# The first stage of a hybrid block in a new written order: two row loads moved, values by halves, roots and exponential steps on GpSimd

## The chip, the cores and the metric

The kernel runs on one core of a Trainium2 chip. Its time is the device time of one execution in microseconds. It has five engines that work side by side, each through its own queue in order: TensorE (PE: matmuls, with weight loads shown as PEld), VectorE (DVE), ScalarE (ACT), GpSimd (POOL) and SyncE (SP), which here issues the loads and stores. They wait for each other through semaphores.

## The reference, cut to what matters

One layer of a model with 512 tokens of width 1024. It norms the input, multiplies it by a wide matrix, runs a state-space branch and an attention branch with compressed, selected and window keys on the result, merges them, and goes on to a feed-forward part and to a gate on a second embedding `p`:

```python
n1 = rmsnorm(h, g_mix[i])
z = n1 @ w_in[i]
y_ssm = s5_mixer(z[..., OFF_SSM:OFF_Q], ...)
y_nsa = nsa_mixer(z[..., OFF_Q:OFF_KV], ...)
...
gate = jax.nn.sigmoid(rmsnorm(h, g_ple[i]) @ w_ple_gate[i])
h = h + gate * (p[i] @ w_ple_proj[i])
```

Three pieces of it are made in the first stage of the kernel: `p @ w_ple_proj` (512x256 by 256x1024), which needs nothing else; the normed input `n1`; and the columns of `z` that hold the attention values and gates (280 of them). The norm is `x * rsqrt(mean(x*x) + eps) * g`. The state-space branch also needs `exp(lam * dt)`, whose modulus is `rho = exp(lr)` with `lr = lre * dt`, and whose angle goes through sine and cosine tables.

## The kernel before, in words

Every fp32 matrix is split in a high part, which TensorE takes as fp32r, and a low part, the rest. A product is three passes: high by high, low by high, high by low. ScalarE copies the high part and VectorE (later in the kernel GpSimd as well) subtracts it to get the low one.

Tokens stand in four tiles of 128 (`qt` 0 to 3), the width in eight blocks of 128 (`k`). The input is loaded twice: as rows (`rows[qt]`, a token on each partition) and transposed (`xT[:, qt]`, the width on the partitions). For a tile, the first stage does this:

- `squared` (L314): ScalarE squares the row and sums it on the way.
- `rooted` (L318 to L322): GpSimd adds eps and raises to the power -0.5, the sum of one tile at a time.
- `spread` (L324): TensorE multiplies the 128 roots by a diagonal matrix, so that they stand along the free dimension of a bank, the same on all partitions.
- `x_scaled` (L329): VectorE multiplies each block of `xT` by its column of gains and by the spread roots, four blocks a half.
- `n_high`, `n_low`: ScalarE copies the high part into `n1h` by halves, VectorE subtracts it to get `n1l` in one instruction a tile.
- `v_passes` (L290): TensorE multiplies the normed tile by the value weights `WV` (high and low, made by `copy(*wv(...))` and `wv_lo`), three passes of eight matmuls.

Ahead of them and between them TensorE does `embedded(i, qt)` (L426): the product of `p` with the half `i` of `w_ple_proj`, six matmuls of 512 columns for each of the eight (`i`, `qt`). `embedded_out` copies each result out of its bank; SyncE stores it to DRAM later. VectorE has small steps besides: `angles()` (L391), a generator of 128x16 instructions that `some(n)` advances, ends with the angle of the state-space poles and gives `lr` after sixteen steps. `exp_of(rho, lr, "e1", G)` gives `rho` on GpSimd, after the stage, where the planner puts it behind `exp_at`. `u_split` splits the weights of the first two projections.

Two rules set the order. Inside `tc.manual_schedule` (L445 to L529) the instructions of TensorE, ScalarE, VectorE and GpSimd keep the order in which they are written, each engine its own. Everything outside is placed by a planner that orders the queues by its own costs; `tc.issue_after(ins)` keeps a block's instructions behind `ins` on its engine. Loads on SyncE keep their written order at the head of the program. Banks of PSUM come in four pairs (`acc`, `s`, `t`, `o`); a matmul into a pair waits until an older user of a bank is read out. `either()` hands out `acc` and `o` in turn.

After the stage, the first of the projections (`proj`, 24 matmuls of 512 columns) multiplies `n1` by 128 columns of `w_in`. It needs all four tiles of `n1h` and `n1l`, and so everything above.

## Time and profile before

| | us |
|---|---|
| median of three runs | 806.93 (806.4 to 807.37) |
| the profiled execution | 806.35 |
| its span, first instruction to last | 804.6 |
| TensorE busy in the span | 789.8 |
| VectorE, ScalarE, GpSimd busy | 515.6, 403.4, 251.0 |
| start of the first projection's matmuls | 34.59 |

Rows of the profile give the start and the length in us, the engine, the line of the kernel, the operation and its output and inputs by name; x8 stands for eight such instructions in a row; the bracket tells how long the engine sat idle before and what ended that. Rows of groups give the busy time and the mean ns of one, then the idle time in front of the group. Rows by stretch give the stretch's length and then each engine's busy time with its count of instructions, the granted TensorE clock, the share of DMA and GB/s. Rows of DMA issues give KB and the us from issue to landing. Most of these operations stand on helper lines (L54 is any `tt`, L58 and L60 any `ts`, L63 any `stt`, L75 any `copy`), so the tile's name tells which it is.

### The profile page before, as it was taken

The page shows a single profiled execution, that of the slowest core. Times are in us where ns is not written, and L with a number is a line of the kernel's source. Part 1 is how long each engine was busy: PE and PEld are TensorE (multiplying, and loading weights), DVE is VectorE, ACT ScalarE, POOL GpSimd, SP SyncE. Part 2 cuts the span into 40 slices and gives each one's busy share as a digit, 9 for nine tenths or more (in the row PEclk, how much of TensorE's full clock was granted, in tenths as well). Part 3 has the DMA queues.
Part 4 walks back from the last instruction along what each step waited for, and adds up shares of the span by engine and source line. Part 5 has one row for each costly group of instructions (what it writes and reads, how often), then busy time and mean ns, then how long its engine had stood idle before and what let it go on. Part 6 is the DMA issues. An engine that isn't in the chain of part 4 may idle for free.

```text
span 804.6 us, 12045 instructions
## 1 busy us (share of the span) xinstructions
PE 789.8 (98%) x4432; PEld 665.4 (83%) x4432; DVE 515.6 (64%) x1082; ACT 403.4 (50%) x747; POOL 251.0 (31%) x289
## 2 busy tenths in 40 slices
PE   8999999999999999999999999999999999999996
PEld 7888888878888888878898888888888888888885
DVE  6898996866677732595454444545544757999753
ACT  6735653366776743344363444443443433584642
POOL 1667222117555534141032333223333200001221
PEclk9999999999999999999999999999999999999999
DMA  9953212133413312334032222233222252515111
GB/s 349 340 178 131 79 52 73 50 105 105 106 54 107 144 60 83 106 131 156 1 132 95 89 105 82 102 105 105 82 102 98 94 174 80 209 66 171 54 52 53
DMA packets 29851, 89.70 MB, mean 111 GB/s; under 512 B 3680, under 2 KB 6112, under 8 KB 29792
## 3 DMA queue, kind: packets, MB, share of 16 engines
q1 hardware_dynamic: 29216, 87.88, 32.1%
q10 hardware_dynamic: 576, 1.05, 0.3%
q8 instruction: 35, 0.57, 0.3%
q14 instruction: 24, 0.20, 0.1%
HBM read 79.48 MB, written 5.24 MB: 105 GB/s over the span
## 4 chain that ended last, share of the span: by engine, by line
PE 90%; DVE 5%; ACT 2%; issue 2%; DMA 0%; POOL 0%; POOLq 0%; ACTq 0%; DVEq 0%
PE pj L82 6%; PE pj L83 6%; PE pj L84 6%; PE ua L83 5%; PE ub L84 5%; PE ua L84 5%; PE ua L82 5%; PE ub L82 5%; PE ub L83 5%; PE p L82 3%; PE p L83 3%; PE p L84 3%; PE sps L1020 2%; PE ptp L1040 2%; PE wo L82 2%; PE wo L83 2%
## 5 line engine op out<-in xcount | busy, mean ns | idle before, releaser
L54 POOL TENSOR_TENSOR wl<-wr,wh 128x1024 fp32r<-128x1024 f32 x39 | 93.7, 2403 | 249.4 <-ACT wh L75 215.7
L75 ACT ACTIVATE wh<-wr 128x1024 fp32r<-128x1024 f32 x88 | 93.2, 1059 | 91.4 <-issue 35.0
L54 DVE TENSOR_TENSOR wl<-wr,wh 128x1024 fp32r<-128x1024 f32 x49 | 64.1, 1309 | 51.9 <-ACT wh L75 51.7
L82 PE MATMUL pj<-n1h,wh 128*128 128x512 f32 x224 | 90.7, 405 | 0.9 <-ACT hid L871 0.6
L83 PE MATMUL pj<-n1l,wh 128*128 128x512 f32 x224 | 87.8, 392 | 0.0
L84 PE MATMUL pj<-n1h,wl 128*128 128x512 f32 x224 | 87.4, 391 | 0.0
L63 DVE SCALAR_TENSOR_TENSOR cv<-ub,cols,cv 128x511 f32<-128x511 f32 (+1 forms) x44 | 32.9, 748 | 66.1 <-ACT cv L1312 65.4
L83 PE MATMUL ua<-n2l,wh 128*128 128x512 f32 (+1 forms) x176 | 66.9, 380 | 0.2 <-DVE n2l L63 0.2
L82 PE MATMUL ua<-n2h,wh 128*128 128x512 f32 (+1 forms) x176 | 66.9, 380 | 0.0
L83 PE MATMUL ub<-n2l,wh 128*128 128x512 f32 (+1 forms) x176 | 66.8, 379 | 0.0
L84 PE MATMUL ub<-n2h,wl 128*128 128x512 f32 (+1 forms) x176 | 66.8, 379 | 0.0
L82 PE MATMUL ub<-n2h,wh 128*128 128x512 f32 (+1 forms) x176 | 66.8, 379 | 0.0
L84 PE MATMUL ua<-n2h,wl 128*128 128x512 f32 (+1 forms) x176 | 66.8, 379 | 0.0
L82 PEld LDWEIGHTS pj<-n1h,wh 128*128 128x128 f32 x224 | 42.1, 188 | 9.4 <-ACT hid L871 0.7
L84 PEld LDWEIGHTS pj<-n1h,wl 128*128 128x128 f32 x224 | 42.1, 188 | 8.9
L83 PEld LDWEIGHTS pj<-n1l,wh 128*128 128x128 f32 x224 | 42.2, 188 | 7.7 <-issue 0.4
L60 POOL TENSOR_SCALAR pr<-pr,su,gates 128x512 f32<-128x512 f32 (+2 forms) x64 | 40.3, 644 | 16.7 <-DVE su L1032 13.2
L54 DVE TENSOR_TENSOR pl<-ptp,ph 128x128 fp32r<-128x128 f32 (+1 forms) x64 | 31.0, 487 | 16.4 <-ACT ph L75 15.2
L75 ACT ACTIVATE ph<-ptp 128x128 fp32r<-128x128 f32 (+1 forms) x64 | 27.7, 435 | 26.9 <-PE ptp L1040 26.7
L83 PEld LDWEIGHTS ua<-n2l,wh 128*128 128x128 f32 x176 | 33.1, 188 | 6.7 <-DVE n2l L63 0.4
L84 PEld LDWEIGHTS ub<-n2h,wl 128*128 128x128 f32 x176 | 33.1, 188 | 6.3
L84 PEld LDWEIGHTS ua<-n2h,wl 128*128 128x128 f32 x176 | 33.1, 188 | 6.2
(481 smaller groups left out, 2014.5 us busy)
## 6 DMA issues: line engine op xcount, KB each, us to landing
wr<-in_w_up_dram SPq DMA_DIRECT2D x44, 512.0 KB, 3.5
wr<-in_w_in_dram SPq DMA_DIRECT2D x28, 512.0 KB, 3.4
b<-in_w_down_dram SPq DMA_DIRECT2D x14, 512.0 KB, 3.6
QQ<-QT SPq DMA_DIRECT2D x16, 256.0 KB, 3.8
wr<-in_w_out_dram SPq DMA_DIRECT2D x8, 512.0 KB, 3.5
wr<-in_w_down_dram SPq DMA_DIRECT2D x8, 512.0 KB, 3.9
wr<-in_w_ple_gate_dram SPq DMA_DIRECT2D x8, 512.0 KB, 3.5
xT<-in_x_t_dram SPq DMA_DIRECT2D x4, 512.0 KB, 9.0
```

The costliest lines, as they stand in the source:

```text
L54: e.tensor_tensor(o, a, b, op=op)
L60: e.tensor_scalar(o, a, s1, s2, op0=op0, op1=op1)
L63: e.scalar_tensor_tensor(o, a, s, b, op0=op0, op1=op1)
L75: S.activation(o, a, AF.Copy)
L82: PE.matmul(ps, lh, rh, start=start, stop=False)
L83: PE.matmul(ps, lh, rl, start=False, stop=False)
L84: PE.matmul(ps, ll, rh, start=False, stop=stop)
L1020: PE.matmul(o, self.QQ[:, x, qt * P:(qt + 1) * P], KK[:, :, self.g, :w] if both else KK[:, self.br, self.g, :w], start=x == 0, stop=x == 1)
L1040: PE.transpose(ps[:, (qt - kt) * P:(qt - kt + 1) * P], self.pr[qt][:, kt * P:(kt + 1) * P], ident)
```

## The change

- Warming: nine matmuls on a tile `heat`, filled by VectorE, in place of six on `ident` and `root`.
- Loads: rows 0 and 1 are issued behind the two loads of the second half of `w_ple_proj`; before, they were issued ahead of them. In both versions they are ahead of the first transposed tile.
- `spread` takes a bank for each tile, not one for all four. The banks of `embedded` and of the value products are named, not handed out in turn.
- `n_low` goes by halves. `v_pass` takes one pass, or half of one; the order of the passes differs from tile to tile, and a tile's passes no longer stand together.
- Tile 3's second half is scaled in two steps: GpSimd multiplies by the gains (`x_times_g`), then VectorE multiplies all four blocks by the spread roots in one instruction.
- Seven GpSimd instructions of the exponential are written after the roots of tiles 0 and 1; the rest after tile 3's gains, inside the written block. Before, all were behind `exp_at`.
- One copy out of a bank (`embedded_out(0, 2)`) is VectorE's. The copies out of banks, the square sums and the value weights come at other places.
- `v_high` and `v_low` of tiles 0 and 1 come after all low parts.
- Outside the block: `FL`'s and `CT`'s copies on ScalarE are held behind the last value copy, and `W2d`'s on GpSimd behind the tables.

```diff
@@ -236,8 +236,10 @@
     rows = [wv0[:, 1].rearrange("p a b -> p (a b)"), *(px.tile([P, D], F32, name=f"row{qt}") for qt in range(1, NQ))]
     root = px.tile([P, P], F32, name="root")
     ts(root, ident, math.sqrt(D), None, MUL, None, G)
-    half = px.tile([P, 1], F32, name="half")
-    G.memset(half, -0.5)
+    heat = px.tile([P, P], F32, name="heat")
+    V.memset(heat, 1.0)
+    expo = px.tile([P, 1], F32, name="expo")
+    G.memset(expo, -0.5)
 
     def rowload(qt):
         nc.sync.dma_start(rows[qt], dr("x", qt * P * D, [[D, P], [1, D]]))
@@ -259,10 +261,10 @@
         nc.sync.dma_start(pin[:, k], dr("p_t", k * T * P, [[T, P], [1, T]]))
         wpload(0, k)
     nc.sync.dma_start(cols, dr("cols", 0, [[NCOLS, P], [1, NCOLS]]))
-    for qt in range(2):
-        rowload(qt)
     for k in range(2):
         wpload(1, k)
+    rowload(0)
+    rowload(1)
     xload(0)
     VV = slot(pa, "v8", [P, NQ, 2, 2, 2, HD], F32R, "VV")
     WV = slot(pa, "kv", [P, 2, KD, 280], F32R, "WV")
@@ -287,14 +289,16 @@
     def wv_lo(i):
         tt(wv(1, i)[0], wv(1, i)[1], wv(0, i)[0], SUB)
 
-    def v_passes(qt, passes):
+    vcount = [0] * NQ
+
+    def v_pass(qt, n, ks=range(KD)):
         if qt not in vps:
-            vps[qt] = bank(either(), "vps")
-        for n in passes:
-            nn, x = ((n1h, 0), (n1l, 0), (n1h, 1))[n]
-            for k in range(KD):
-                PE.matmul(vps[qt][:, :280], nn[:, k, qt * P:(qt + 1) * P], WV[:, x, k], start=n + k == 0,
-                          stop=n == 2 and k == KD - 1)
+            vps[qt] = bank("ot"[qt // 2] if qt != 1 else "acc", "vps")
+        nn, x = ((n1h, 0), (n1l, 0), (n1h, 1))[n]
+        for k in ks:
+            PE.matmul(vps[qt][:, :280], nn[:, k, qt * P:(qt + 1) * P], WV[:, x, k], start=vcount[qt] == 0,
+                      stop=vcount[qt] == 3 * KD - 1)
+            vcount[qt] += 1
 
     def v_high(qt):
         S.activation(gates[:, qt], vps[qt][:, 256:280], AF.Tanh, scale=0.5)
@@ -319,33 +323,32 @@
 
         r = rx[qt] = small("rx")
         ts(r, ss4[:, qt:qt + 1], D * EPS, None, ADD, None, G)
-        tt(r, r, half, ALU.pow, G)
+        tt(r, r, expo, ALU.pow, G)
 
     def spread(qt):
-        if not rbp:
-            rbp[0] = bank("s", "rb")
-        PE.matmul(rbp[0][:, qt * P:(qt + 1) * P], rx[qt].to_broadcast([P, P]), root, start=True, stop=True)
+        rbp[qt] = bank("s", "rb")
+        PE.matmul(rbp[qt][:, :P], rx[qt].to_broadcast([P, P]), root, start=True, stop=True)
+
+    def x_times_g(qt, half):
+        for k in range(4 * half, 4 * half + 4):
+            ts(xT[:, qt, k], xT[:, qt, k], gmix[:, k:k + 1], e=G)
 
     def x_scaled(qt, half):
+        if qt == 3 and half:
+            x = xT[:, qt, 4 * half:4 * half + 4]
+            tt(x, x, rbp[qt][:, None, :P].to_broadcast([P, 4, P]), MUL)
+            return
         for k in range(4 * half, 4 * half + 4):
-            stt(xT[:, qt, k], xT[:, qt, k], gmix[:, k:k + 1], rbp[0][:, qt * P:(qt + 1) * P], MUL, MUL)
-
-    def n_of(qt, half):
-        ks = slice(4 * half, 4 * half + 4)
-        return (slice(None), ks, slice(qt * P, qt * P + P)), xT[:, qt, ks]
+            stt(xT[:, qt, k], xT[:, qt, k], gmix[:, k:k + 1], rbp[qt][:, :P], MUL, MUL)
+
+    def n_of(x, qt, half):
+        return x[:, 4 * half:4 * half + 4, qt * P:qt * P + P]
 
     def n_high(qt, half):
-        o, x = n_of(qt, half)
-        copy(n1h[o], x)
-
-    def n_low(qt):
-        o = (slice(None), slice(None), slice(qt * P, qt * P + P))
-        tt(n1l[o], xT[:, qt], n1h[o], SUB)
-
-    def normed_tile(qt):
-        for half in range(2):
-            x_scaled(qt, half)
-            n_high(qt, half)
+        copy(n_of(n1h, qt, half), xT[:, qt, 4 * half:4 * half + 4])
+
+    def n_low(qt, half):
+        tt(n_of(n1l, qt, half), xT[:, qt, 4 * half:4 * half + 4], n_of(n1h, qt, half), SUB)
 
     uw = []
 
@@ -425,28 +428,31 @@
 
     def embedded(i, qt, passes=range(3), ks=range(2)):
         if (i, qt) not in pjb:
-            pjb[i, qt] = bank("t" if i and qt < 2 else either(), "pje")
+            pjb[i, qt] = bank("t" if i and qt < 2 else ("o", "acc")[qt % 2], "pje")
         for k in ks:
             for n in passes:
                 PE.matmul(pjb[i, qt], pT[int(n == 1)][:, k, qt * P:(qt + 1) * P], wp[i][:, int(n == 2), k], start=n + k == 0,
                           stop=n + k == 3)
 
-    def embedded_out(i, qt):
+    def embedded_out(i, qt, e=None):
         n = 4 * i + qt
-        if n == 0:
+        if not pjs:
             pjs.append(slot(pa, "v4", [P, 2, 512], F32, "pjs0"))
             pjs.append(wv0[:, 1].rearrange("p (k a) b -> p k (a b)", k=2))
         elif n == 4:
             t = slot(pS, "Uc", [P, 4, 512], F32, "pjs2")
             pjs.extend((t[:, :2], t[:, 2:]))
         pjo[i, qt] = pjs[n // 2][:, n % 2]
-        copy(pjo[i, qt], pjb[i, qt])
+        if e is None:
+            copy(pjo[i, qt], pjb[i, qt])
+        else:
+            e.tensor_copy(pjo[i, qt], pjb[i, qt])
 
     with tc.manual_schedule(engines={mybir.EngineType.PE, mybir.EngineType.Activation, mybir.EngineType.DVE,
                                     mybir.EngineType.Pool}):
         warm = bank("s", "warm")
-        for _ in range(6):
-            PE.matmul(warm[:, :P], ident, root, start=True, stop=True)
+        for _ in range(9):
+            PE.matmul(warm[:, :P], heat, heat, start=True, stop=True)
         angled = angles()
 
         def some(n):
@@ -458,70 +464,100 @@
             copy(wp[0][:, 0, k], wpr[:, 0, k])
             tt(pT[1][:, k], pin[:, k], pT[0][:, k], SUB)
             tt(wp[0][:, 1, k], wpr[:, 0, k], wp[0][:, 0, k], SUB)
-        squared(0)
+        rho_steps = exp_of(rho, lr, "e1", G)
+
+        def some_rho(n):
+            for _ in range(n):
+                next(rho_steps, None)
+
         for k in range(2):
             for n in range(3):
                 for qt in range(NQ):
                     embedded(0, qt, (n,), (k,))
-        rooted(0)
-        some(16)
-        squared(1)
-        rooted(1)
+        some(7)
         for k in range(2):
             copy(wp[1][:, 0, k], wpr[:, 1, k])
             tt(wp[1][:, 1, k], wpr[:, 1, k], wp[1][:, 0, k], SUB)
-        for qt in range(2):
-            embedded_out(0, qt)
+        some(9)
+        k4 = (range(4), range(4, 8))
+        squared(0)
         embedded(1, 0)
+        rooted(0)
+        squared(1)
         spread(0)
+        embedded_out(0, 2, V)
+        embedded_out(0, 0)
+        embedded_out(0, 1)
+        rooted(1)
+        some_rho(5)
         embedded(1, 1)
+        copy(*wv(0, 0))
         x_scaled(0, 0)
         n_high(0, 0)
-        embedded_out(0, 2)
         x_scaled(0, 1)
+        embedded(1, 2)
         n_high(0, 1)
-        embedded_out(0, 3)
-        embedded(1, 2)
-        n_low(0)
-        copy(*wv(0, 0))
         wv_lo(0)
+        n_low(0, 0)
+        n_low(0, 1)
+        spread(1)
         copy(*wv(0, 1))
         wv_lo(1)
+        x_scaled(1, 0)
+        squared(2)
+        embedded_out(1, 0)
+        embedded_out(0, 3)
+        n_high(1, 0)
+        x_scaled(1, 1)
+        n_high(1, 1)
+        squared(3)
+        rooted(2)
         embedded(1, 3)
+        embedded_out(1, 2)
+        n_low(1, 0)
+        v_pass(0, 0)
+        v_pass(0, 1)
+        v_pass(0, 2)
+        n_low(1, 1)
+        v_pass(1, 0, k4[0])
+        spread(2)
+        v_pass(1, 0, k4[1])
+        x_scaled(2, 0)
+        v_pass(1, 2)
+        x_scaled(2, 1)
+        rooted(3)
+        v_pass(1, 1)
+        spread(3)
+        x_times_g(3, 1)
+        embedded_out(1, 1)
+        n_high(2, 0)
+        x_scaled(3, 0)
+        v_pass(2, 0, k4[0])
+        n_high(2, 1)
+        v_pass(2, 0, k4[1])
+        n_low(2, 0)
+        n_low(2, 1)
+        x_scaled(3, 1)
+        u_split(0, 0)
+        n_high(3, 0)
+        n_high(3, 1)
+        v_pass(2, 2)
+        v_pass(3, 0, k4[0])
+        v_pass(2, 1)
+        v_pass(3, 2)
+        n_low(3, 0)
+        n_low(3, 1)
+        v_pass(3, 1)
+        v_pass(3, 0, k4[1])
+        u_split(0, 1)
+        embedded_out(1, 3)
+        some_rho(50)
         for qt in range(2):
-            embedded_out(1, qt)
-        spread(1)
-        v_passes(0, (0, 1))
-        squared(2)
-        rooted(2)
-        normed_tile(1)
-        v_passes(0, (2,))
-        n_low(1)
-        for qt in (2, 3):
-            embedded_out(1, qt)
-        spread(2)
-        v_passes(1, (0,))
-        squared(3)
-        rooted(3)
-        normed_tile(2)
-        v_passes(1, (1, 2))
-        n_low(2)
-        v_high(0)
-        u_split(0, 0)
-        exp_at = last(mybir.EngineType.Pool)
-        spread(3)
-        v_passes(2, (0,))
-        normed_tile(3)
-        v_passes(2, (1, 2))
-        n_low(3)
-        v_high(1)
-        v_low(0)
-        v_low(1)
-        u_split(0, 1)
+            v_high(qt)
+            v_low(qt)
         some(50)
         trig_at = last(mybir.EngineType.DVE)
         u_split(1, 0)
-        v_passes(3, (0, 1, 2))
         for qt in (2, 3):
             v_high(qt)
             v_low(qt)
@@ -567,9 +603,6 @@
     for i, m in enumerate(MS):
         G.memset(mt[:, i:i + 1], m)
     sh8 = (P, 8, NPAIR)
-    with tc.issue_after(exp_at):
-        for _ in exp_of(rho, lr, "e1", G):
-            pass
     mtb = mt[:, :, None].to_broadcast(list(sh8))
     ang, aq, az, asn, acs, at = (st(n, sh8) for n in ("ang", "aq", "az", "asn", "acs", "at"))
     tt(ang, kk[:, None, :].to_broadcast(list(sh8)), mtb, MUL)
@@ -646,8 +679,9 @@
         tt(bb[:, 1], bb[:, 1], bt, ADD)
     FL = slot(pa, "ptc", [P, 2, 16, 2, NCMP], F32, "FL")
     for i in range(2):
-        copy(FL[:, i, :, :, NCMP - 1], pes[:, i, :, None].to_broadcast([P, 16, 2]))
-        S.activation(CT[:, i], bcraw[:, 2 + i], AF.Copy, scale=(1.0, -1.0)[i])
+        with tc.issue_after(zero_at):
+            copy(FL[:, i, :, :, NCMP - 1], pes[:, i, :, None].to_broadcast([P, 16, 2]))
+            S.activation(CT[:, i], bcraw[:, 2 + i], AF.Copy, scale=(1.0, -1.0)[i])
 
     tt(RC[0], rho4, COS[:, 7], MUL)
     tt(RC[1], rho4, SIN[:, 7], MUL)
@@ -826,7 +860,8 @@
     nc.sync.dma_start(W2[:, 0], dr("cmp_wk2", 0, [[HD, P], [1, HD]]))
     nc.sync.dma_start(W2[:, 1], dr("cmp_wv2", 0, [[HD, P], [1, HD]]))
     W2d = pa.tile([P, 2, HD], F32, name="W2d")
-    G.tensor_copy(W2d, W2[:, 0:1].to_broadcast([P, 2, HD]))
+    with tc.issue_after(tab_at):
+        G.tensor_copy(W2d, W2[:, 0:1].to_broadcast([P, 2, HD]))
     KK = slot(pa, "kv", [P, 2, 2, T], F32R, "KK")
     KC = pa.tile([P, 2, 2, 64], F32R, name="KC")
     with tc.issue_after(tab_at):
```

## The prediction

> **What bounds the kernel now.** I read the page first, then the busy time by stretch, then TensorE's timeline of the first stretch with its waits, then the other engines in that stretch. On the page and by stretch:
>
> ```profile
> PE 789.8 (98%) x4432; PEld 665.4 (83%) x4432; DVE 515.6 (64%) x1082; ACT 403.4 (50%) x747; POOL 251.0 (31%) x289
> ```
> ```profile
> 0.00:34.60 34.60, 29.72 (x165) 26.27 (x166) 24.56 (x66) 23.85 (x45) 11.32 (x42) 1.00 0.96 369
> 34.60:90.00 55.40, 55.40 (x314) 46.29 (x313) 48.43 (x119) 30.38 (x55) 37.59 (x74) 1.00 0.44 148
> ```
>
> TensorE is busy 789.8 of 804.6 us. The first 34.6 us hold 4.9 of its 14.8 idle us, and the 55 us behind them none: the first projection opens at 34.59 and TensorE never stops until 90. So whatever brings that first projection forward is kept, as long as the engines that feed it come forward too. TensorE's timeline (start, us, engine, line) and its waits in the first 120 us:
>
> ```profile
> 2.21 2.93 PE L449 MATMUL warm<-root,ident 128*128 128x128 f32 x12 [2.21 <-POOL mt L568]
> 4.87 2.07 PE L431 MATMUL pje<-wp,pTh 128*128 128x512 f32 x4
> ...
> 8.05 1.98 PE L431 MATMUL pje<-wp,pTh 128*128 128x512 f32 x8
> ...
> 18.86 1.30 PE L296 MATMUL vps<-WV,n1h 128*128 128x280 f32 x8 [1.11 <-ACT WV L75]
> ...
> 33.56 1.20 PE L296 MATMUL vps<-WV,n1h 128*128 128x280 f32 x8
> 34.59 0.40 PE L82 MATMUL pj<-n1h,wh 128*128 128x512 f32 x1
> ```
> ```profile
> PE vps L296 <- DVE n1l L54: 1.3, 3, 0.5
> PE vps L296 <- ACT WV L75: 1.1, 1, 1.1
> PE wbps L755 <- ACT WB L75: 0.6, 1, 0.6
> PE pj L82 <- ACT hid L871: 0.6, 1, 0.6
> ```
>
> Two things are to be seen. The first is a matmul's price: four 512-column ones in 2.07 at 4.87 are 0.43 each with the last one's tail left out; eight in 1.98 at 8.05 are 0.227. Single records put the change at 7.6:
>
> ```profile
> 7.17 1.04 PE L431 MATMUL pje<-wp,pTl 128*128 128x512 f32 x3
> ```
>
> These three start 0.42 and 0.23 apart. A pass of eight 280-column ones takes 1.03 (33.56 to 34.59). The second is the floor of this stage: 48 embedding matmuls x 0.227 = 10.9, 12 value passes x 1.03 = 12.4, four spreads at 0.22 = 0.9, together 24.2 us. From 4.87 that ends at 29.1; the stage ends at 34.59. Of the 5.5 us between, 1.4 is the slow clock (2.7 us at half speed). The rest is waits from 17.75 on: 1.1 for the value weights, 1.3 for low parts, and some more that the tails of the matmuls in front hide, as each tail counts as busy for 0.16.
>
> **What feeds it.** Rows of ScalarE, then VectorE's and ScalarE's groups by shape from 12 to 34.6:
>
> ```profile
> 8.13 1.06 ACT L314 ACTIVATE wv<-wv 128x1024 f32<-128x1024 f32 x1 [1.19 <-DMA wv<-in_x_dram]
> 9.43 1.06 ACT L314 ACTIVATE row<-row 128x1024 f32<-128x1024 f32 x1 [0.15 <-DMA row<-in_x_dram]
> 10.49 1.14 ACT L75 ACTIVATE wp<-wpr 128x512 fp32r<-128x512 f32 x2
> ...
> 16.66 2.15 ACT L75 ACTIVATE WV<-wv 128x1024 fp32r<-128x1024 f32 x2
> ...
> 25.89 0.71 ACT L650 ACTIVATE CT<-bcraw 128x256 f32<-128x256 f32 x2
> ...
> 35.15 1.15 ACT L710 ACTIVATE Z<-ident 128x512 f32<-128x512 f32 x2
> ...
> 40.10 1.06 ACT L75 ACTIVATE wh<-wr 128x1024 fp32r<-128x1024 f32 x1 [0.26 <-ACT CX L710]
> ```
> ```profile
> L63 DVE SCALAR_TENSOR_TENSOR xT<-xT,cols,rb 128x128 f32<-128x128 f32 x32 | 8.6, 341 | 1.0 <-PE rb L327 1.0
> L54 DVE TENSOR_TENSOR n1l<-xT,n1h 128x1024 fp32r<-128x1024 f32 x4 | 4.9, 1225 | 2.9 <-ACT n1h L75 2.9
> L54 DVE TENSOR_TENSOR WV<-wv,WV 128x1216 fp32r<-128x1216 f32 x1 | 1.4, 1418 | 0.0
> L54 DVE TENSOR_TENSOR WV<-wv,WV 128x1024 fp32r<-128x1024 f32 x1 | 1.2, 1226 | 0.2 <-ACT WV L75 0.2
> L54 DVE TENSOR_TENSOR wl<-wr,wh 128x1024 fp32r<-128x1024 f32 x1 | 1.2, 1216 | 0.0
> ```
> ```profile
> L75 ACT ACTIVATE n1h<-xT 128x512 fp32r<-128x512 f32 x8 | 5.0, 630 | 4.4 <-DVE xT L63 4.4
> ```
>
> Scale, copy high, subtract low is a ring between two engines: VectorE waits 2.9 us for the high copies, ScalarE 4.4 us for the scaled tiles, TensorE 1.3 us for the low parts. VectorE is the longest of the three: 32 scalings (8.6), 4 low parts (4.9), two value-weight low parts (2.6) and wl (1.2) are 17.3 us of work, from 13.46 on, and first wl ends at 34.18.
>
> **The change, part by part.**
>
> Warm matmuls: nine on a tile that VectorE fills, not six on `root`. They lose the 2.21 us wait for GpSimd and can begin near 1.1 (no row; the other engines' first rows lie at 0.8 and a fill takes 0.1 to 0.2). Nine are 18 entries of 0.213 (12 entries fill 2.21 to 4.87), so they end at 4.9, when the first embedding operand is there. In this run the doubling came 5.4 us after the first matmul; 5.4 after 1.1 is 6.5, and 1.1 us of slow clock less saves 0.5 us. Bounds: no earlier than the old 7.6 (nothing saved), or at once (1.2 saved).
>
> By the Trainium skill, "TensorE: Matmul & The Clock Gate", section on the HAM clock gate, the gate opens after one busy window of 3413 ns that runs free of the kernel, so it would open anywhere from 4.5 to 7.9 here, which an estimate from that page makes 0 to 0.9 us of the same stage. The one transition in this trace lies within it and can't tell.
>
> Loads: the two rows go behind the second half of `w_ple_proj`. Issues and times to landing:
>
> ```profile
> 4.07 0.98 SPq L256 DMA_DIRECT2D wpr<-in_w_ple_proj_dram  x2
> 5.10 0.69 SPq L246 DMA_DIRECT2D xT<-in_x_t_dram  x1
> 5.83 1.12 SPq L272 DMA_DIRECT2D wv<-in_w_v_dram  x2
> ```
> ```profile
> wpr<-in_w_ple_proj_dram SPq DMA_DIRECT2D x2, 256.0 KB, 6.1
> ```
> ```profile
> xT<-in_x_t_dram SPq DMA_DIRECT2D x1, 512.0 KB, 6.9
> ```
> ```profile
> wv<-in_w_v_dram SPq DMA_DIRECT2D x1, 608.0 KB, 8.2
> ```
>
> Rows landed at 8.1 and 9.4, the weights at 10.1 and 10.7, x at 12.0, the second value weights at 14.6: about 1.3 us per 512 KB. After: weights 7.5 and 8.1, rows 9.4 and 10.7, x and all behind it unmoved, as the bytes ahead are the same. So the rows, which the title puts ahead, come 1.3 us later; they were ahead of x before too.
>
> First scaling: row 0 squared 9.4 to 10.5 (1.15 as between the rows 8.13 and 9.43), root to 11.5. For the root and the GpSimd work after it:
>
> ```profile
> 9.68 0.57 POOL L54 TENSOR_TENSOR rx<-rx,half 128x1 f32<-128x1 f32 x1
> ...
> 30.83 0.25 POOL L58 TENSOR_SCALAR gtFalse<-e1n 128x16 f32<-128x16 f32 x1
> 31.17 1.29 POOL L54 TENSOR_TENSOR e1r<-gtFalse,e1r 128x16 f32<-128x16 f32 x1
> ```
> ```profile
> 13.46 2.15 DVE L63 SCALAR_TENSOR_TENSOR xT<-xT,cols,rb 128x128 f32<-128x128 f32 x8 [1.02 <-PE rb L327]
> ...
> 31.15 1.22 DVE L54 TENSOR_TENSOR n1l<-xT,n1h 128x1024 fp32r<-128x1024 f32 x1 [0.70 <-ACT n1h L75]
> ...
> 39.70 0.18 DVE L54 TENSOR_TENSOR rho<-rho 128x16 f32<-128x16 f32 x1 [1.42 <-POOL rho L54]
> ...
> 57.58 1.71 DVE L54 TENSOR_TENSOR wl<-wr,wh 128x1024 fp32r<-128x1024 f32 x1
> ```
>
> TensorE reaches the spread at 12.5 (24 matmuls with six still slow, then six more), so scaling starts at 12.95, against 13.46. VectorE gets one copy out of a bank ahead of it, at 12.05, as wide as half a low part and taken at its 0.6, and the split of the 16 small steps costs nothing new.
>
> From there I walk VectorE in the new order, each item at the start-to-start time of its rows (scaling 0.26 an eighth, half a low part 0.60, value low parts 1.14 and 1.33): tile 0 scaled to 15.0; value low part 16.2; two half low parts 17.4; value low part 18.7; tile 1 scaled to 20.8; its low parts to 22.2; tile 2 scaled to 24.2; half of tile 3 to 25.6; low parts of tile 2 to 26.8; the other half of tile 3 as one 512-wide product 27.4; its low parts 28.9; wl 30.0. It waits under 1.1 us on the way, since each wait for a high copy has another item in it. The same walk over the old order ends in 34.5 for a measured 34.59, so its constants are sound.
>
> TensorE: value pass 0 starts at 17.05 (weights copied to 16.9, earlier because ScalarE leaves four bank copies for later), three passes to 20.1; tile 1's first half waits 0.4 and second half 0.3; from 24.4 no wait over 0.15; last pass ends at **30.7**. The first projection has wh (25.9), wl (30.0) and a free bank (28.6). That is 3.9 us ahead.
>
> Products by the gain on GpSimd: four of 128x128, unseen in the old trace. Nearest rows: 0.25 for a 128x16 one (30.83), from below; from above 1.29, for one that runs into a VectorE low part (31.17). They start behind the fourth root, at 23.6, and VectorE wants them at 26.8: 0.5 each ends at 25.6, harmless; 1.29 each ends at 28.8 and costs 2.0 on VectorE, about 1.7 on TensorE. I take the low end, because VectorE is then scaling out of a bank, as it was at 30.83.
>
> The row at 31.17 against that at 31.15 shows GpSimd held until the low part is over, and wl at 57.58 shows VectorE paying 0.5 when GpSimd is dense. GpSimd's steps towards rho, now about 25.6 to 31.5 rather than up to 39.6, meet six two-operand items; half an average step each is 0.7 us, part of it in TensorE's slack: **0.4 us**.
>
> The Trainium skill, "SBUF — State Buffer", section on the two sides, speaks against this part: a VectorE instruction with two SBUF inputs and a GpSimd one lock each other out for the whole instruction. The two rows agree. By the rule at its worst six waits of 0.25 make 1.5 us, and the sum would be 0.7 lower than mine.
>
> Moved work: the table copies to `FL` and `CT`, about 1 us of ScalarE, go behind the last value copy. There ScalarE needs 31.3 to 36.0 for its eight zero fills (35.15 to 39.84, where the wait ahead of 40.10 begins), so wh of the third projection starts near 37.0, not 36.3; its matmuls are due at 41.6, so it costs nothing. Without that cover it would cost 0.7. `W2d` costs 0.3 of idle GpSimd. rho is ready before the angle tables start, so VectorE's 1.42 us wait is gone, but TensorE didn't wait for that.
>
> **Sum.** 3.9 less 0.4 is 3.5 us. The profiled execution took 806.35 (span 804.6), so it would take 802.85; the median of the runs is 0.58 above it, so against the median it is **803.4**, which I predict.
>
> **Rivals.** *Half of it*: the gate opens late (0.6) and GpSimd's products run into low parts (0.9 more): the projection opens at 32.6, gain 2.0, **804.9**. For it: the row of 1.29. Against: the products fall into scalings.
> *No change*: everything outside the written block is placed anew. A gain of 3.5 is used up if the state-space quarters behind the projections keep their place because VectorE's chain of tables and products does: **806.9**. For it: VectorE works 48.4 of the 55.4 us ahead of 90. Against: TensorE waits for nothing there, and the chain on VectorE starts earlier as well.
> *Slower*: the new placement puts one projection ahead of the first quarter's scans instead of beside them. TensorE then stands for what these 24 matmuls covered, 24 x 0.227 = 5.4 us: 803.4 + 5.4 = **808.8**. It decides from 3.5 us on, two thirds of a projection. For it: the waits of 0.6 on WB and on hid, TensorE's only ones from 34.6 to 120, lie in that stretch. Against: nothing in the edit asks for another order.
> *The order isn't what sets it*: if the stage is bound by loads, the opening stays within 1 us of 34.6: 806. The last load it needs lands near 22, so I give it little.
>
> **How the numbers follow.** Forecast (802.4 to 804.4) 0.55, better than that 0.03, half 0.17, no change or load-bound 0.12, slower 0.13. A measurement of this kernel can tell about 0.2%, 1.6 us, from no change; so faster takes forecast, better and nearly all of half, 0.74; slower the last, 0.13; the rest is the same. The range goes from 801.9, all unknown costs at their best ends, to 806.5, into the no-change case; some 2 in 10 lie outside, mostly above. The forecast's own range is 802.4 to 804.4.
>
> **What would show it.** First projection between 30.7 and 31.6 (32.6 for half); warm matmuls from about 1.1 and a doubling before 7; first value pass near 17; VectorE idle under 1.5 us from 13 to 30 with the products for tile 3 done before 26.8; TensorE without a wait to about 86. I am wrong if the projection opens early and the time doesn't follow, or if VectorE stands for GpSimd before tile 3's second half.

## The result and the profile after

The changed kernel takes 802.68 us (median of six runs, 802.32 to 803.35) against 806.97 for the kernel before (six runs, 806.4 to 807.37): a ratio of 0.9946 with a 95% interval of 0.9934 to 0.9958, 4.3 us faster. The profiled execution took 802.63, its span is 800.9; between the two profiled spans lie 3.7 us, as the old one's execution was 0.6 us under its median and the new one's is at its own.

Busy time by stretch of the changed kernel (length, then TensorE, its weight loads, VectorE, ScalarE, GpSimd, each with its count; clock, DMA share, GB/s):

```profile
0.00:34.60 34.60, 33.41 (x189) 29.70 (x190) 28.51 (x84) 26.19 (x51) 18.16 (x58) 1.00 0.97 374
34.60:90.00 55.40, 54.96 (x309) 45.60 (x309) 47.57 (x111) 28.45 (x50) 32.18 (x62) 1.00 0.45 148
```

TensorE was busy 29.7 us of the first 34.6 and is now busy 33.4: 3.7 us more work is done by then. The next stretch, which had no idle time, has 0.44 us. The timeline of TensorE in the first stage:

```profile
1.11 4.04 PE L455 MATMUL warm<-heat 128*128 128x128 f32 x18 [1.11 <-DVE heat L240]
4.90 1.20 PE L434 MATMUL pje<-wp,pTh 128*128 128x512 f32 x4
...
11.85 0.48 PE L330 MATMUL rb<-root,rx 128*128 128x128 f32 x2
...
16.67 1.29 PE L299 MATMUL vps<-WV,n1h 128*128 128x280 f32 x8
...
29.29 0.40 PE L82 MATMUL pj<-n1h,wh 128*128 128x512 f32 x1
29.52 0.39 PE L83 MATMUL pj<-n1l,wh 128*128 128x512 f32 x1
29.76 0.68 PE L299 MATMUL vps<-WV,n1l 128*128 128x280 f32 x4
30.27 0.68 PE L299 MATMUL vps<-WV,n1h 128*128 128x280 f32 x4
30.79 0.40 PE L84 MATMUL pj<-n1h,wl 128*128 128x512 f32 x1
```

From 4.90 on no row has a bracket: TensorE waits for nobody in this stage. The first four embedding matmuls take 1.20, not 2.07: the time of a matmul halves near 4.9 us here, and did near 7.6 before. The planner moved the first two matmuls of the projection ahead of the last eight value matmuls, so 29.29 is not the whole stage's end. The third one, at 30.79, is the measure: two matmuls of 0.227 before it is 30.3, against 34.59 before. The stage is 4.3 us shorter.

VectorE and ScalarE from 12 to 34.6, in groups by shape (busy, mean ns, then the idle time ahead):

```profile
L63 DVE SCALAR_TENSOR_TENSOR xT<-xT,cols,rb 128x128 f32<-128x128 f32 x28 | 7.6, 340 | 0.6 <-PE rb L330 0.6
L54 DVE TENSOR_TENSOR n1l<-xT,n1h 128x512 fp32r<-128x512 f32 x8 | 5.3, 688 | 0.2
```
```profile
L75 ACT ACTIVATE n1h<-xT 128x512 fp32r<-128x512 f32 x8 | 4.9, 626 | 1.8 <-DVE xT L54 1.2 <-DVE xT L63 0.6
```

VectorE's wait for the high copies went from 2.9 us to 0.2, ScalarE's for scaled tiles from 4.4 to 1.8. The work is nearly the same, with 0.4 us more for low parts in halves.

A new wait stands at 63 us. TensorE, then VectorE, then GpSimd in that place, and last the same product `z` on VectorE in the kernel before:

```profile
63.60 0.50 PE L82 MATMUL pj<-n1h,wh 128*128 128x512 f32 x1 [0.44 <-DVE QT L54]
```
```profile
61.07 1.87 DVE L54 TENSOR_TENSOR z<-PI,bb 128x256 f32<-128x256 f32 x1
62.86 0.68 DVE L54 TENSOR_TENSOR QT<-pj,QT 128x512 fp32r<-128x512 f32 x1
```
```profile
61.24 0.72 POOL L54 TENSOR_TENSOR x<-PR,CT 128x320 f32<-128x320 f32 x1
61.93 0.73 POOL L54 TENSOR_TENSOR x<-PI,CT 128x320 f32<-128x320 f32 x1
```
```profile
64.97 0.42 DVE L54 TENSOR_TENSOR z<-PI,bb 128x256 f32<-128x256 f32 x1
```

A projection needs the bank that VectorE empties with a query tile's low part (`QT`). Ahead of that stands one product `z` of the state-space tables, which took 1.87 us here and 0.42 before: it began at 61.07 and came out only when two GpSimd products of the other tables had ended.

### The profile page after: what moved, and what is told of

The parts are those of the page before. It is cut to its first block, busy times and chain, and to the rows that moved or that the text cites. A ratio compares the mean times of both kernels' runs of the same rounds, so it can differ in the third digit from the quotient of the medians.

```text
span 800.9 us, 12064 instructions
## 1 busy us (share of the span) xinstructions
PE 789.4 (99%) x4438; PEld 665.1 (83%) x4438; DVE 515.8 (64%) x1085; ACT 402.9 (50%) x746; POOL 252.2 (31%) x293
## 4 chain that ended last, share of the span: by engine, by line
PE 88%; DVE 4%; DMA 3%; issue 2%; ACT 2%; SPq 0%; POOL 0%; POOLq 0%; ACTq 0%; DVEq 0%
PE pj L82 6%; PE pj L83 6%; PE pj L84 6%; PE ua L83 5%; PE ub L84 5%; PE ua L84 5%; PE ub L83 5%; PE ua L82 5%; PE ub L82 5%; PE p L84 3%; PE p L83 3%; PE p L82 3%; PE sps L1055 2%; PE ptp L1075 2%; PE wo L82 2%
## 5 line engine op out<-in xcount | busy, mean ns | idle before, releaser
L83 PEld LDWEIGHTS ub<-n2l,wh 128*128 128x128 f32 x176 | 33.0, 188 | 6.3
```

Source lines behind the costliest of these rows:

```text
L83: PE.matmul(ps, lh, rl, start=False, stop=False)
```

## The experiments

Four theories were put against each other. *Order*: the gain comes from the written order, in which every wait of the ring between VectorE, ScalarE and TensorE has other work in it. *Clock*: it comes from warming TensorE earlier. *Cleared queues*: it comes from keeping foreign instructions (`FL`, `CT`, `W2d`, the exponential) out of the block's queues. *Rows*: it comes from when the rows land. Each run was timed beside the kernel before on the same chip, in five rounds. The experiments ran on three chips, on which the kernel before took 806.63 to 806.99, so differences of a few tenths are read from the ratios. In the table, "value matmuls" is the start of the last row of value matmuls in the profiled execution, "row 0" the start of its square sum. A row of eight ends 0.5 us further behind its start than one of four. In the new order two matmuls of the projection stand ahead of that row, in `low_whole` one.

| kernel | median us | ratio to before, 95% interval | value matmuls | row 0 |
|---|---|---|---|---|
| before | 806.97 | | 33.56 (eight) | 8.13 |
| changed | 802.68 | 0.9946 (0.9934 to 0.9958) | 30.27 | 9.65 |
| warm_only | 806.54 | 1.0000 (0.9991 to 1.0009) | 33.71 (eight) | 8.51 |
| old_warm | 803.15 | 0.9953 (0.9941 to 0.9966) | 31.64 | 9.96 |
| holds_only | 806.85 | 1.0004 (0.9995 to 1.0013) | 34.01 (eight) | 8.78 |
| no_holds | 802.69 | 0.9948 (0.9936 to 0.9961) | 31.15 | 10.52 |
| rows_first | 804.58 | 0.9969 (0.9958 to 0.9979) | 32.44 | 11.66 |
| whole_passes | 803.88 | 0.9961 (0.9948 to 0.9973) | 30.83 (eight) | 9.63 |
| low_whole | 803.30 | 0.9959 (0.9945 to 0.9972) | 30.71 | 9.72 |
| stt_all | 803.35 | 0.9956 (0.9943 to 0.9968) | 31.18 | 10.44 |
| rho_late | 804.08 | 0.9966 (0.9954 to 0.9978) | 30.41 | 9.67 |
| rho_late_z | 802.71 | 0.9949 (0.9937 to 0.9962) | 30.73 | 9.68 |
| z_hold | 802.90 | 0.9948 (0.9935 to 0.9960) | 31.14 | 10.38 |
| pad10 | 805.71 | 0.9985 (0.9976 to 0.9993) | 30.64 | 9.94 |

### The warm matmuls, alone and taken back

`warm_only` is the kernel before with the new warm matmuls:

```diff
-        for _ in range(6):
-            PE.matmul(warm[:, :P], ident, root, start=True, stop=True)
+        for _ in range(9):
+            PE.matmul(warm[:, :P], heat, heat, start=True, stop=True)
```

> The kernel before with the new warm matmuls alone. Theory order (the gain comes from the new order of the ring between VectorE, ScalarE and TensorE): the old order's first spread waits for VectorE's low part of the second embedding weights at 12.4 us, which no clock moves, so the first projection opens at 34.4 instead of 34.6 and the time is 0.0 to 0.4 us under before. Theory clock (the gain is the earlier opening of the clock gate): the stage gets the 1.3 us of slow matmuls back and more, 2 us or more under before.

`old_warm` is the changed kernel with the same lines turned back, and no `heat`.

> The changed kernel with the old warm matmuls (six on ident and root, which wait for GpSimd until 2.2 us). Theory order: TensorE is now what bounds the stage, so matmuls at half speed until 5.6 to 8 us cost 0.3 to 1.2 us: the first projection opens at 30.7 to 31.5, and the time is 3.0 to 4.0 us under before. Theory clock: 2 us or less under before.

Alone it is worth 0.1 us, which no measurement tells from nothing (ratio 1.0000). Its embedding matmuls run fast earlier, but the old order lets nobody use it: the profile has the same waits as before, and one more, of TensorE on a weight of the second half of `w_ple_proj`.

```profile
PE pje L433 <- ACT wp L75: 0.5, 1, 0.5
PE vps L298 <- DVE n1l L54: 1.2, 3, 0.5
PE vps L298 <- ACT WV L75: 1.1, 1, 1.1
PE warm L451 <- DVE heat L240: 1.1, 1, 1.1
```

Taken back from the changed kernel it costs 0.5 us in the medians, within the intervals of the two. The profiled stage ends 1.4 us later (31.64 against 30.27). Its first eight embedding matmuls are slow where the changed kernel has fast ones; the first four of them:

```profile
4.96 2.07 PE L432 MATMUL pje<-wp,pTh 128*128 128x512 f32 x4
```

Theory clock is out for all but about half a microsecond, as the gain is 3.5 us without the new warming. Of the 1.4 us, 0.4 is given back near 63, where this run has no wait on `QT`.

### The holds outside the block, alone and taken back

`holds_only` puts the `issue_after` lines for `FL`, `CT` and `W2d` into the kernel before; `no_holds` takes them out of the changed one:

```diff
-        with tc.issue_after(zero_at):
-            copy(FL[:, i, :, :, NCMP - 1], pes[:, i, :, None].to_broadcast([P, 16, 2]))
-            S.activation(CT[:, i], bcraw[:, 2 + i], AF.Copy, scale=(1.0, -1.0)[i])
+        copy(FL[:, i, :, :, NCMP - 1], pes[:, i, :, None].to_broadcast([P, 16, 2]))
+        S.activation(CT[:, i], bcraw[:, 2 + i], AF.Copy, scale=(1.0, -1.0)[i])
...
-    with tc.issue_after(tab_at):
-        G.tensor_copy(W2d, W2[:, 0:1].to_broadcast([P, 2, HD]))
+    G.tensor_copy(W2d, W2[:, 0:1].to_broadcast([P, 2, HD]))
```

> The kernel before with FL's and CT's copies held behind the last value copy and W2d behind the tables. Theory order: they stood for 0.9 us on ScalarE, of which only CT's 0.6 between two high copies is on the ring: 0.1 to 0.3 us under before. Theory cleared queues (the gain comes from keeping foreign instructions out of the block): 2 us or more under before.

> The changed kernel without these holds, so that the planner may put FL, CT and W2d anywhere. Theory order: the planner puts them into ScalarE's queue inside the block, up to 1 us there, of which the ring has some slack: 3.3 to 4.3 us under before. Theory cleared queues: 2.5 us or less under before.

Neither moves the time: 0.2 us slower alone, 0.0 us when taken back, though without the holds the copies do stand among ScalarE's work of the stage (`FL` at 17.64, `CT` at 26.77). This half of theory cleared queues is out; the exponential is the other half, below.

### The loads in the old order

```diff
-    for k in range(2):
-        wpload(1, k)
     rowload(0)
     rowload(1)
+    for k in range(2):
+        wpload(1, k)
```

> The changed kernel with the loads in the old order (both rows ahead of the second half of w_ple_proj), everything else as changed. Theory order: ScalarE's written order takes the second half's weights (landing at 10.1 and 10.7) ahead of the square sums, so the first root comes 1.3 us later, the first scaling starts near 14.4 and the first projection opens near 32.2: 2.0 to 3.0 us under before. Theory rows (rows that land early are what counts): the same as the changed kernel or better, 4.3 us under before or more.

804.58: 1.9 us of the gain are gone, as theory order expected, and its runs (803.69 to 805.1) don't overlap with the changed kernel's. The square sum of row 0 begins at 11.66, though the row landed at 8.5: ScalarE's written order has the weights ahead of it. TensorE waits for the first root:

```profile
PE rb L330 <- POOL rx L54: 0.7, 1, 0.7
```

So the loads are worth having in the order in which ScalarE's queue uses them. Theory rows, by which a row that lands earlier is better, is out.

### The passes whole, the low parts whole, and the gains on VectorE

`whole_passes` gives TensorE the value products as before, pass by pass and tile by tile; the other engines keep the new order:

```diff
-        v_pass(1, 0, k4[0])
         spread(2)
-        v_pass(1, 0, k4[1])
+        v_pass(1, 0)
...
-        v_pass(2, 2)
-        v_pass(3, 0, k4[0])
         v_pass(2, 1)
-        v_pass(3, 2)
+        v_pass(2, 2)
+        v_pass(3, 0)
         n_low(3, 0)
         n_low(3, 1)
         v_pass(3, 1)
-        v_pass(3, 0, k4[1])
+        v_pass(3, 2)
```

> The changed kernel with the value products as whole passes in the order of before (high by high, low by high, high by low; tile by tile), VectorE, ScalarE and GpSimd as changed. Theory order, by the walk of the queues: the first projection opens at 31.3 to 31.6, TensorE waits for each tile's low part again: 3.0 to 3.5 us under before. If TensorE's order is worth nothing: 4.3 us under before. If it is most of the gain: 2 us or less.

1.2 us slower than the changed kernel and 3.0 under the kernel before, as theory order expected. TensorE waits for a low part again, though once and not for each tile, and longer than in any of the three waits before:

```profile
PE vps L299 <- DVE n1l L54: 0.6, 1, 0.6
```

`low_whole` makes each tile's low part in one instruction behind both high copies:

```diff
     def n_low(qt, half):
-        tt(n_of(n1l, qt, half), xT[:, qt, 4 * half:4 * half + 4], n_of(n1h, qt, half), SUB)
+        if half:
+            tt(n1l[:, :, qt * P:qt * P + P], xT[:, qt], n1h[:, :, qt * P:qt * P + P], SUB)
```

> The changed kernel with each tile's low part in one instruction, behind both halves' high copies, all else as changed. By the walk TensorE's passes over low parts come later and the first projection opens at 31.2 to 31.5: 0.6 to 1.1 us above the changed kernel, 3.2 to 3.7 us under before. If the order of the passes alone covers it: within 0.2 us.

0.6 us slower in the medians and 1.0 by the ratios, as expected, though the run ranges overlap (803.14 to 803.98 against 802.32 to 803.35).

`stt_all` scales tile 3's second half on VectorE, four instructions like the others, without GpSimd's products:

```diff
-        x_times_g(3, 1)
...
-        if qt == 3 and half:
-            x = xT[:, qt, 4 * half:4 * half + 4]
-            tt(x, x, rbp[qt][:, None, :P].to_broadcast([P, 4, P]), MUL)
-            return
```

> The changed kernel with tile 3's second half scaled by four VectorE instructions like all others, without the GpSimd products. By the walk of the queues VectorE is 0.45 us later from there and TensorE has that much slack: the first projection opens within 0.2 us of the changed kernel, 4.0 to 4.4 us under before. If VectorE set the end of the stage, 0.4 to 0.6 us above the changed kernel.

0.7 us slower in the medians, where 0.2 was expected; the run ranges overlap (802.60 to 803.77), and so do the intervals of the ratios. VectorE doesn't set the end of the stage: at nearly the same landing of row 0 the last value matmuls start at 31.18, as in `no_holds` (31.15). VectorE also reaches the place near 63 as it does there: its `wl` ahead of `z` starts at 60.40, in `no_holds` at 60.36. What differs is `z` itself, 1.87 us against 0.95, and the wait on `QT` that `no_holds` has not:

```profile
64.42 0.50 PE L82 MATMUL pj<-n1h,wh 128*128 128x512 f32 x1 [0.35 <-DVE QT L54]
```

Whether the edit brings that about, or the profiled execution happened to meet it, isn't shown. So what the products on GpSimd are worth stays open: no difference beyond the noise is shown.

### The exponential late, and the wait on QT taken away

`rho_late` puts the exponential on GpSimd outside the block again, behind tile 3's gains:

```diff
-        some_rho(5)
...
         x_times_g(3, 1)
+        exp_at = last(mybir.EngineType.Pool)
...
-        some_rho(50)
...
+    with tc.issue_after(exp_at):
+        for _ in rho_steps:
+            pass
```

> The changed kernel with the exponential on GpSimd outside the block again, behind the gains of tile 3. Theory order: GpSimd's steps only meet VectorE's low parts at another time, the first projection opens within 0.3 us of the changed kernel: 4.0 to 4.6 us under before, and VectorE may wait for rho again without TensorE waiting. Theory cleared queues: rho's early start is what the rest of the kernel gains from, 3 us or less under before.

1.4 us slower, with run ranges that don't overlap (803.68 to 804.75), and with the stage unchanged (30.41 against 30.27). Its TensorE row near 63, and VectorE's rows for rho and near 63:

```profile
64.42 0.50 PE L82 MATMUL pj<-n1h,wh 128*128 128x512 f32 x1 [1.14 <-DVE QT L54]
```
```profile
36.73 0.18 DVE L54 TENSOR_TENSOR rho<-rho 128x16 f32<-128x16 f32 x1 [1.99 <-POOL rho L54]
...
61.90 1.87 DVE L54 TENSOR_TENSOR z<-PI,bb 128x256 f32<-128x256 f32 x1
63.69 0.68 DVE L54 TENSOR_TENSOR QT<-pj,QT 128x512 fp32r<-128x512 f32 x1
```

VectorE waits 1.99 us for rho, its tables are 0.8 us later at 61.90, and TensorE's wait on `QT` grows from 0.44 to 1.14. Theory order had this as free, theory cleared queues as 1.3 us or more: here the latter is right, though 2.8 us of the gain remain without it. To see whether that place is the whole of it, `rho_late_z` adds one more hold, and `z_hold` adds it to the changed kernel: the first products `z` have to stay behind the low part of the query tile.

```diff
...
         high_at.append(last(mybir.EngineType.Activation))
+        sub_at.append(last(mybir.EngineType.DVE))
...
-                with tc.issue_after(low_at[late + 2] if e is V else tab_at):
+                with tc.issue_after(low_at[late + 2] if e is V else tab_at), tc.issue_after(sub_at[late] if e is V else tab_at):
```

> The late exponential (outside the block, as before) together with that hold. Theory VectorE takes the rest: the late exponential cost its 1.4 us through the same wait alone (VectorE stands 2.0 us for rho, so the low part came 0.8 us later), so with the hold it is within 0.3 us of the run with the hold alone, 4.3 to 5.1 us under before. If the late exponential costs somewhere else, it stays 1 us or more behind that run.

> The changed kernel with the first products of the state-space tables on VectorE held behind the low part of the first query tile; on VectorE that low part moves ahead of two products and nothing else moves. Theory VectorE takes the rest (the changed kernel's first stage gains 4.3 us, and 0.4 to 0.8 of it is lost near 63 us, where TensorE waits for that low part to free its bank): the wait goes and the time is 0.3 to 0.8 us under the changed kernel, 4.6 to 5.1 under before. If another engine sets that place: within 0.2 us of the changed kernel.

With the hold, the late exponential costs nothing: 802.71, as the changed kernel. In its profile VectorE still waits 1.99 us for rho, but TensorE has no wait near 63; the low part now comes first:

```profile
61.91 0.68 DVE L54 TENSOR_TENSOR QT<-pj,QT 128x512 fp32r<-128x512 f32 x1
62.51 0.58 DVE L54 TENSOR_TENSOR z<-PR,bb 128x256 f32<-128x256 f32 x1
63.02 0.95 DVE L54 TENSOR_TENSOR z<-PI,bb 128x256 f32<-128x256 f32 x1
```

So rho's price goes through the order of `z` and the low part at that place. In the two profiled executions the longer wait is 0.7 of the 1.1 us between the spans and the stage 0.1; the rest isn't placed. But the hold doesn't make the changed kernel faster (802.90 against 802.68, no difference): that part of the expectation failed. Its profiled execution has no wait, but its value matmuls start at 31.14, 0.9 us after those of the changed kernel, as row 0 came at 10.38 there and not at 9.65.

Whether an execution without the hold meets the wait depends on how GpSimd's two products fall. In the changed kernel, `rows_first`, `low_whole`, `stt_all` and `rho_late` they begin 0.17 us behind `z`, `z` takes 1.87, and TensorE waits 0.34 to 1.14 us. In `no_holds`, `old_warm` and `whole_passes` `z` takes 0.42 to 1.09, and there is no wait. (In `pad10` TensorE waits 0.31 with a `z` of 0.41, behind a `wl` of 1.75.) It isn't a matter of being late: `rows_first`, the latest of them without `pad10`, has the wait, and `no_holds`, which comes earlier, has not. How often the changed kernel's other executions meet it isn't known, since one is profiled; if it is seldom, the hold has little to win.

### What a microsecond of the stage is worth

`pad10` adds ten matmuls that nobody reads behind the value products:

```diff
+        pad = bank("s", "pad")
+        for k in range(10):
+            PE.matmul(pad[:, :512], pT[0][:, 0, 0:P], wp[1][:, 0, 0], start=True, stop=True)
```

> The changed kernel with ten 512-column matmuls into a spare bank behind the value products, whose result nobody reads. It prices how a microsecond of the first stage reaches the end. Theory order (what the stage gains is kept one for one): 10 x 0.227 = 2.3 us above the changed kernel, 1.6 to 2.3 us under before. If something later sets the end, under 1 us above the changed kernel.

The spans differ by 2.6 us (803.5 against 800.9) and the medians by 3.0, for 2.3 us of matmuls. That is about one for one, with an uncertainty of 1.2 us from the two ratios' intervals. Against the kernel before it is 1.2 us faster, where 1.6 to 2.3 was expected. Nothing behind the stage absorbs time that is added to it, but for the wait on `QT`, which an execution meets or not.

All the profiled spans can be cut at the first spread and at the end of the stage (the start of the first matmul behind the value products, less 0.227 for each matmul of the projection ahead of it):

| kernels | first spread | from it to the end of the stage | rest of the span | wait on `QT` in it |
|---|---|---|---|---|
| before, warm_only, holds_only | 13.0 to 13.6 | 21.4 to 21.6 | 769.9 to 770.1 | none |
| old_warm, no_holds, z_hold, rho_late_z | 12.5 to 13.4 | 18.3 to 18.5 | 769.9 to 770.1 | none |
| changed | 11.85 | 18.5 | 770.6 | 0.44 |
| pad10 without its ten matmuls | 12.4 | 18.3 | 770.5 | 0.31 |
| stt_all | 12.6 | 18.6 | 770.7 | 0.35 |
| low_whole | 12.3 | 18.7 | 770.5 | 0.34 |
| rows_first | 13.8 | 18.7 | 770.9 | 0.44 |
| whole_passes | 11.9 | 19.5 | 770.2 | none |
| rho_late | 11.9 | 18.6 | 771.5 | 1.14 |

So of the 3.7 us between the two spans, 1.2 come from an earlier first spread, 3.1 from there to the end of the stage, and 0.5 are lost behind it. The middle part is there with the old warm matmuls and without the holds too: it is what the new order in the stage is worth, with the banks that go with it. The first part moves with the clock and with the landing of row 0 from one execution to the next. No run gives VectorE alone its old order back, so that the placing of its items is the larger part is argued from the waits that went, not shown.

## Why the prediction was right, and where it wasn't

Forecast 803.4, measured 802.68: inside the range and the forecast's own 802.4 to 804.4. Step by step:

- **The bound.** The claim that VectorE's ring set the stage, and that the floor of TensorE's matmuls lay 5.5 us below its end, held: with the ring's waits filled, TensorE runs from 4.90 on without a wait and ends 1.2 us above that floor (30.3 against 29.1).
- **The walk.** It had the first spread at 12.5 and the end of the stage at 30.7, 18.2 us later; the profiles of the new order have 18.3 to 18.7 (`whole_passes` aside). In the changed kernel's profile the stage ended at 30.3 because the first spread came at 11.85, and that was luck: the clock doubled near 4.9 there. In `rho_late_z`, where it doubled near 6.3 and row 0 came as early (9.68), the first spread is at 12.50 and the stage ends at 30.8.
- **The price of the shared port.** The 0.4 us added for it, which made 31.1, is the term that was mis-sized. VectorE's eight half low parts took 688 ns on average, as the one of the same shape at 4.09 did (0.69), when GpSimd was idle; only 0.2 us of idle time lay ahead of them. GpSimd did the waiting: beside `wl`, which took no longer than elsewhere, a step of it took 1.10 us that took 0.25 at 30.15:

```profile
28.41 1.24 DVE L54 TENSOR_TENSOR wl<-wr,wh 128x1024 fp32r<-128x1024 f32 x1
```
```profile
28.66 1.10 POOL L58 TENSOR_SCALAR gtFalse<-e1q 128x16 f32<-128x16 f32 x1
```

- **Warm matmuls.** Start 1.1 (measured 1.11), end 4.9 (4.9). The doubling was put at 6.5 and came near 4.9 in this profile, between 4.3 and 7.2 in those of the new warming. The saving was put at 0.5, and `old_warm` is 0.5 us slower, within its uncertainty. By the prediction's own figures a doubling at 4.9 instead of 7.6 saves half of 2.7 us, 1.4, where it writes 1.2 and, for a doubling from 4.5 on, 0.9.
- **Loads.** Rows at 9.4 and 10.7 were expected; the first square sum starts at 9.65. That the rows come later by the change was read rightly (the title says only that they move). That this order is worth 1.9 us by itself was not said; only the walk contained it.
- **First scaling.** 12.95 was expected; it starts at 12.37, half a microsecond earlier, behind the earlier first spread.
- **GpSimd's gains.** Put at 0.5 each, they took 0.6: 2.38 us for four, from 23.01 to 25.39, needed at 26.42. The low end was the right choice, but the row given for it was misread: at 30.83 VectorE was not scaling, it was idle ahead of 31.15. The GpSimd rows that do fall into that scaling (28.30 to 30.45) are those from 28.54 to 30.24, 0.20 to 0.29 each, so the argument holds by them.

```profile
23.01 2.38 POOL L58 TENSOR_SCALAR xT<-xT,cols 128x128 f32<-128x128 f32 x4
```

- **Moved copies.** Costed at nothing, and worth nothing in both directions. ScalarE reached the third projection's wh at 36.79 (37.0 expected).
- **rho.** Here a step failed: "VectorE's 1.42 us wait is gone, but TensorE didn't wait for that". TensorE didn't wait for it in the old kernel, where it came later to the place concerned. With TensorE 4 us earlier, VectorE's chain of tables is next to set the time, and rho late costs 1.4 us in the medians, 0.7 of it seen as a longer wait.
- **What comes next.** "TensorE without a wait to about 86" was wrong: it waits at 63. The prediction had the mechanism of the lost microseconds (VectorE held by a dense GpSimd) but put it into the stage, while it struck at 61 us.
- **The sum.** It had 3.9 less 0.4, 3.5 us. In the profiled executions the stage gained 4.3 and 0.5 was lost behind it, 3.7 us in all: that this is so near is partly luck, an early clock and a price paid elsewhere than forecast. In the medians the gain is 4.3, as the old profiled execution lay 0.6 under its median and the new one at its own.
- **Rivals.** In the changed kernel's profile the late gate didn't come; in that of `no_holds` it did, near 7 us, without undoing the gain. The slow products didn't come. The planner kept the order behind the stage (TensorE's waits of 0.6 on WB and hid stand as before), so the slower case had no ground. The no-change case had the right engine, VectorE's chain between 34 and 86, but it takes back 0.5 us and not 3.5.

## What to carry to other kernels

When a stage is a ring of engines, count each engine's work and put into every wait an item of another tile or weight; here that took TensorE's idle time behind the warm matmuls from 2.7 us to 0.1, while the pieces without the order (warming, holds) are worth nothing alone. Loads belong in the order in which the in-order queue that uses them asks for them, worth 1.9 us here. After such a gain look at once for the next engine's chain: work off the path in the old profile, such as rho, can be on it in the new one. And cut the profiles at a point behind the chance of loads and clock, here the first spread, before comparing two kernels by one execution each.

## What the runs showed of the hardware that was not expected

**The clock gate opens at no fixed time.** The gate shows here as the time of a 512-column matmul, 0.43 us at first and 0.227 later. With the same nine warm matmuls from 1.11 on, the first four embedding matmuls took 1.20 in the changed kernel (fast from the start) and 2.05 in `rows_first` (slow throughout):

```profile
4.97 2.05 PE L434 MATMUL pje<-wp,pTh 128*128 128x512 f32 x4
```

In the profiles of the eleven kernels with the new warming, the time from one matmul to the next halves at the earliest between 4.25 and 4.43 us (`rho_late`) and at the latest between 6.82 and 7.22 (`rows_first`), 3.1 to 6.1 us after the first matmul; in the three with the old one between 7.6 and 8.4. The Trainium skill ("TensorE: Matmul & The Clock Gate", section on the HAM clock gate) says that the gate looks at windows of 3413 ns that run free of the kernel. The spread of 2.4 to 3.0 us, less than one window, agrees with that; the earliest opening is 0.1 to 0.3 us ahead of what a full busy window would allow.

**One VectorE instruction can be held through two GpSimd instructions.** `z` at 61.07 took 1.87 us, as long as the two GpSimd products from 61.24 to 62.66 and its own 0.4 together, and so in four more profiles in which they begin 0.17 us behind it; in `no_holds`, where one of them was under way, the same instruction took 0.95, and 0.42 in the kernel before, where they began after it. That they hold it is read from these times; no run moves the products alone. The Trainium skill ("SBUF — State Buffer", section on the two sides) has a lock for the whole instruction of the other engine. Here the price was two in a row, which the prediction's 0.25 to 0.5 per meeting doesn't cover.

**The same load lands up to 0.9 us apart.** Row 0, with the same loads ahead of it, was there at 9.65 in the changed kernel and at 10.52 in `no_holds`, by the start of its square sum. With the clock, this moved the first spread, and the end of the stage with it, by about a microsecond between these profiles (11.85 and 12.76), so that single profiles of kernels that differ by less than that have to be compared from the first spread on.
